# First head group's queries and keys as two interleaved sets of seven products, in a fused decoder layer on one core

## The chip, the cores and the metric

The kernel runs on one core of a Trainium2 chip. Its time is the device time of one execution in microseconds; the figure compared is the median over several runs. A profiled execution gives the trace from which all single durations come.

## The reference

One layer (batch 1, 512 positions, model width 1024, float32) with three branches that mix positions, gates, and a convolutional feed-forward network:

```python
u = rmsnorm(x, ln1_g)
proj = u @ w_in
q, k, v, pool_in, z, xbc, dt_raw, gate_pre = jnp.split(proj, split_idx, axis=-1)
y_a = dilated_attention_mixer(q, k, v, rel_bias) @ w_a        # 3 groups of 6 heads of 64
y_b = pool_mixer(pool_in, pool_w, pool_scale) @ w_b           # causal means over 2, 4, 8, 16
y_c = ssd_mixer(z, xbc, dt_raw, ...) @ w_c
gates = jax.nn.sigmoid(gate_pre + b_gate)
x = x + (gates[0] * y_a + gates[1] * y_b + gates[2] * y_c) @ w_o
x = x + conv_ffn(rmsnorm(x, ln2_g), ...)
return rmsnorm(x, final_g)
```

The change touches how the columns of `proj` for the first head group's queries and keys are computed: q and k of group 0 are each a product of u (512 x 1024) with 384 columns of `w_in`. Everything else is computed as before.

## The kernel before

**Products.** Every float32 operand is split into a high part (a cast to the format fp32r) and a low part (the operand less its high part). A product is three passes of TensorE: high weights by high x, high weights by low x, low weights by high x (`mm3`, L234). The normed x lies turned, with the model width on the partitions, as `uh` and `ul` in eight blocks of 128 rows by 512 positions. Most projections go by `chunk_a`: a tile of 128 columns of the weights is one accumulation of 3 x 8 matmuls of 128 x 512.

**Jobs and what runs ahead.** The work is a list of jobs, each a block of weights of up to 1 MB and a body with the matmuls. At the start of job n, VectorE makes the low part of the block of job n+1 (`wl`, L215), ScalarE is set to cast block n+2 (`wh`, L195), and SyncE's queue fetches block n+3 (`raw`, two buffers). TensorE, ScalarE, VectorE and GpSimd execute in the order in which the program is written; the DMA issues on SyncE's queue are ordered by the framework. Small pieces of other work (items) run between the products: `step()` advances each item in `running` to its next `yield`, and `after(n, item)` lets n steps pass first.

**The start.** x is loaded, its rows are normed and turned by TensorE, 256 positions at a time; `begin` (L1817) multiplies the first two weight blocks with each half as it comes. These two blocks and the two that follow, `weights[2]` and `weights[3]`, are the projections of the pool branch: eight chunks of 128 columns, two in a block. Each chunk is drained by `pool_evac`: ScalarE copies it out (`pu`, L926), GpSimd adds shifted copies (`psw`, L930 to L933: one addition for chunks 0 and 1, two for 2 and 3, three for 4 and 5, four for 6 and 7, with small copies beside them), and some steps later the item `later` makes the difference `pd` on VectorE (L939), its high part `pdh` on ScalarE (L941) and its low part `pdl` on VectorE (L942). Behind the pool projections come the values of group 0 (two jobs, matmuls of 128 x 400, tile `pb`), the queries and keys of group 0 (`qk_jobs(0)`, three jobs with a `q` and a `k` tile each, tile `pqk`), the pool's own products (`ppw`), the attention of group 0, and the output of the pool branch.

**Sevens.** The queries and keys of group 1 and some gates go by a scheme of Strassen's kind (`set_of_sevens`): the model width is cut into two halves of 4 blocks, the positions into two halves (`LO`, `HI`) and the columns into two sides, lefts (queries) and rights (keys). Seven products, named one to seven, of half the width, half the positions and one side's columns each take the place of eight. Each is, for each 128 columns of the side, 3 x 4 matmuls of 128 x 256. They need sums and differences of the quarters of x (`sums_of_u`: two `uf` that rebuild a block from its parts, four sums `sa` and `sb`, their high parts on ScalarE and low parts `sal`, `sbl` on VectorE; kept in `US`) and of the weights (`w`, L349, held in a pool `ypool` of two buffers). The sums of x are made once, during the output of the pool branch. The results are put together as they are drained: ScalarE copies `one`, `five`, `six` and `seven` out (L742), VectorE makes queries from `two` and keys from `six` and `seven` (the sinks, `q_sink` and `k_sink`, L694).

Of the kernel before, what the change touches and what calls it, by code (L numbers as in the profile page):

```python
# [13 lines left out]
OP = mybir.AluOpType  # L14
AX = mybir.AxisListType

P = 128
# [66 lines left out]
def trunk(ctx: ExitStack, tc, out, x, rel_bias, ln1_g, w_in, b_gate, w_a, pool_w, pool_scale, w_b,  # L84
# [469 lines left out]
    def grouped(ap, g):  # L554

        return ap.rearrange("p (r j) -> p r j", r=4)[:, :, ::-1]
# [4 lines left out]
    def plain(ap, g):  # L561
        return ap if g == 0 else ap.rearrange("p (r j) -> p r j", r=4)
# [114 lines left out]

    def q_sink(g, c):
        t = QK["q", g, c] = T(f"q{g}")
        half = lambda hi: grouped(t, g)[:, :, 64 * hi:64 * hi + 64]  # L680

        def two(ps, r):
            dve.scalar_tensor_tensor(half(0), turned_(ps), 0.125, turned_(r), OP.mult, OP.add)

        def four(ps):
            act.mul(half(1), turned_(ps), 0.125)

        return two, four

    def k_sink(g, c):  # L690
        t = QK["k", g, c] = T(f"k{g}")

        def put(hi, a, b):
            dve.tensor_tensor(plain(t, g)[:, :, 64 * hi:64 * hi + 64], turned_(a), turned_(b),  # L694
                              OP.subtract)

        return put

    def turned_(ap):
        return ap.rearrange("p (j r) -> p r j", r=4)  # L700

    ROLE, turn_of, due = {}, [0], []
# [7 lines left out]
    def set_of_sevens(lefts, rights, x, scales=(1.0, 1.0)):  # L710

        q = lambda two, c0: w_in[:, c0:c0 + P].rearrange("(k two p) c -> two p k c", two=2, p=P)[two]
        cols = [[c for c, _ in side] for side in (lefts, rights)]
        W, r, sinks = [], {}, {}
        role = {"two": "y", "five": "b", "three": "b"}

        def load():
            w = ypool.tile([P, 4, S], F32, name="w3", tag="xs")
            for h in range(2):
                W.append(w[:, :, 256 * h:256 * h + 256])  # L720
                for j, src in enumerate(quarter(0, h)):
                    sp.dma_start(W[h][:, :, src[0]:src[1]], src[2])

        def quarter(two, h):
            if cols[h][1] == cols[h][0] + P:
                c = cols[h][0]
                return [(0, 256, w_in[:, c:c + 256].rearrange("(k two p) c -> two p k c", two=2, p=P)[two])]
            return [(j * P, j * P + P, q(two, cols[h][j])) for j in range(2)]

        def bank(which):  # L730
            if not ROLE:
                for n in ("c", "y", "a", "b"):
                    ROLE[n] = MM("p")
            return ROLE[which]

        def cut(t, j):
            return t[:, 256 * j:256 * j + 256]

        def copy(ps, name, scales=(1.0, 1.0)):
            t = r[name] = T(name)  # L740
            if scales[0] == scales[1]:
                act.mul(t, ps, scales[0])  # L742
            else:
                for j in range(2):
                    act.mul(cut(t, j), cut(ps, j), scales[j])
            return t

        def use(name, ps):
            if name in ("two", "six"):
                for j, (_, make) in enumerate(lefts if name == "two" else rights):  # L750
                    sinks[name == "six", j] = make()
            if name == "one":
                copy(ps, "one", scales)
            elif name == "five":
                copy(ps, "five")
            elif name == "two":
                for j in range(2):
                    sinks[0, j][0](cut(ps, j), cut(r["one"], j))
            elif name == "six":
                t = copy(ps, "r2")  # L760
                for j in range(2):
                    sinks[1, j](0, cut(bank("b"), j), cut(t, j))
            elif name == "seven":
                t = copy(ps, "r7")
                for j in range(2):
                    sinks[1, j](1, cut(r["five"], j), cut(t, j))
            elif name == "four":
                for j in range(2):
# [19 lines left out]
        return load, sevens(lambda two, h: [src for _, _, src in quarter(two, h)], 256, W, body)  # L788

    def attend(g):  # L790
        nm, ls = both[:, :, :HEADS], both[:, :, 32:]
# [130 lines left out]
    def pool_evac(m, ps):  # L922
        g = m // 2
        w = 2 << g
        u = T("pu")
        act.copy(u, ps)  # L926
        cur, sh = u, 1
        while sh < w:
            nxt = T("psw")
            pool.tensor_tensor(nxt[:, sh:], cur[:, sh:], cur[:, :S - sh], OP.add)  # L930
            pool.tensor_copy(nxt[:, :sh], cur[:, :sh])
            cur, sh = nxt, sh * 2
        pool.tensor_tensor(cur[:, :w], cur[:, :w], ramp[:, g, :w], OP.mult)  # L933

        def later():
            yield
            yield
            d = T("pd")
            dve.scalar_tensor_tensor(d, cur, 1.0 / w, u, OP.mult, OP.subtract)  # L939
            dh, dl = T("pdh", F32R), T("pdl", F32R)  # L940
            act.copy(dh, d)  # L941
            dve.tensor_sub(dl, d, dh.bitcast(F32))  # L942
            DP[m] = (dh, dl)

        running.append(later())
# [1023 lines left out]
```

## Time and profile before

| | |
|---|---|
| median of 3 runs | 1025.87 us (1025.46 to 1026.5) |
| the profiled execution | 1026.25 us, its span 1024.5 us |
| mean granted TensorE clock | 0.998 |
| TensorE busy | 1014.8 us, 5396 matmuls |
| VectorE busy | 706.2 us, 967 instructions |
| ScalarE busy | 489.8 us, 821 instructions |
| GpSimd busy | 175.5 us, 143 instructions |

The span runs from the first to the last instruction of the profiled execution; its own time is 1.75 us longer. PE is TensorE's matrix engine, PEld its loading of weights (beside the matmuls), DVE is VectorE, ACT ScalarE, POOL GpSimd, SP SyncE. A timeline row gives start and busy time in us, engine, line, operation, output and inputs by their names in the program, shape, type, the count of instructions in the row, and in brackets the idle time ahead of it with what ended it.

### The profile page before, as it was taken

The numbers are of one execution on the slowest core, as the hardware profiler recorded it, in microseconds if no ns is written. First come the engines' busy times: TensorE is split into PE (matmuls) and PEld (weight loads), VectorE is DVE, ScalarE is ACT, GpSimd is POOL, SyncE is SP. The second block draws the span as 40 slices with busy tenths as digits, with TensorE's granted clock in tenths as the row PEclk, the third lists the DMA queues.
The fourth block names the chain that finished last, engine by engine and source line by source line (L and its number), as shares of the span: only waits on it lengthen the run. The fifth ranks groups of instructions, "written<-read, shape, count | busy, mean of one in ns | idle before, by whom it ended". The sixth has DMA issues, their size and how long they took to land.

```text
span 1024.5 us, 13696 instructions
## 1 busy us (share of the span) xinstructions
PE 1014.8 (99%) x5396; PEld 862.2 (84%) x5396; DVE 706.2 (69%) x967; ACT 489.8 (48%) x821; POOL 175.5 (17%) x143
## 2 busy tenths in 40 slices
PE   9999999999999999999999999999999999999997
PEld 9988878899998888888888888898888888888885
DVE  5562566776857758766768769767768677666775
ACT  6432455355546564567455235554454443443342
POOL 2680000011100004210143611202111011111120
PEclk9999999999999999999999999999999999999999
DMA  8444222147454234552253879342233224323142
GB/s 271 136 120 149 89 76 76 31 99 190 104 134 124 83 110 117 144 133 59 78 156 129 279 140 277 123 139 88 83 124 122 85 82 164 123 84 122 63 144 82
DMA packets 123055, 126.30 MB, mean 123 GB/s; under 512 B 5715, under 2 KB 104342, under 8 KB 122991
## 3 DMA queue, kind: packets, MB, share of 16 engines
q1 hardware_dynamic: 118015, 118.02, 36.8%
q0 software_dynamic: 4384, 6.55, 4.1%
q8 instruction: 42, 0.69, 0.3%
q10 hardware_dynamic: 592, 0.86, 0.2%
q14 instruction: 22, 0.18, 0.0%
HBM read 119.53 MB, written 2.22 MB: 119 GB/s over the span
## 4 chain that ended last, share of the span: by engine, by line
PE 95%; DVE 2%; DMA 1%; ACT 1%; issue 0%; ACTq 0%; DVEq 0%
PE pa L234 32%; PE pu L234 22%; PE p L234 19%; PE pqk L234 6%; PE pb L234 4%; PE pa L1817 2%; PE ps L813 1%; PE pu L1601 1%; PE ppw L234 1%; PE pt L841 1%; PE po L854 1%; PE py L1139 1%; DMA vr<-v 1%; DMA xin<-in_x_dram 1%; DVE wl L215 1%; PE pyo L1146 1%
## 5 line engine op out<-in xcount | busy, mean ns | idle before, releaser
L215 DVE TENSOR_TENSOR wl<-raw,wh 128x2048 fp32r<-128x2048 f32 (+3 forms) x89 | 196.8, 2212 | 40.4 <-ACT wh L195 31.0
L195 ACT CAST wh<-raw 128x1024 fp32r<-128x1024 f32 (+3 forms) x176 | 170.8, 991 | 43.4 <-DVE raw L339 26.1
L1462 DVE SCALAR_TENSOR_TENSOR hc<-pu,fcol,hc 128x510 f32<-128x510 f32 x88 | 65.8, 748 | 61.5 <-ACT hc L1459 59.8
L234 PE MATMUL pa<-uh,wh 128*128 128x512 f32 x336 | 86.5, 399 | 0.0
L234 PE MATMUL pu<-uh,wl 128*128 128x512 f32 (+1 forms) x352 | 83.7, 380 | 0.0
L234 PE MATMUL pu<-uh,wh 128*128 128x512 f32 (+1 forms) x352 | 83.5, 379 | 0.0
L234 PE MATMUL pu<-ul,wh 128*128 128x512 f32 (+1 forms) x352 | 83.5, 379 | 0.0
L234 PE MATMUL pa<-ul,wh 128*128 128x512 f32 x336 | 83.0, 389 | 0.0
L234 PE MATMUL pa<-uh,wl 128*128 128x512 f32 x336 | 83.0, 389 | 0.0
L1467 POOL TENSOR_TENSOR hc<-hc 128x512 f32<-128x512 f32 x22 | 32.3, 1468 | 272.7 <-DVE hc L1462 237.9
L234 PEld LDWEIGHTS pu<-uh,wl 128*128 128x128 f32 x352 | 64.1, 188 | 12.8 <-DVE wl L215 0.3
L234 PEld LDWEIGHTS pu<-ul,wh 128*128 128x128 f32 x352 | 64.2, 188 | 12.5
L234 PEld LDWEIGHTS pu<-uh,wh 128*128 128x128 f32 x352 | 64.1, 188 | 12.4
L234 PEld LDWEIGHTS pa<-ul,wh 128*128 128x128 f32 x336 | 63.1, 188 | 13.3
L234 PEld LDWEIGHTS pa<-uh,wl 128*128 128x128 f32 x336 | 63.1, 188 | 13.1
L234 PEld LDWEIGHTS pa<-uh,wh 128*128 128x128 f32 x336 | 61.2, 188 | 12.7 <-issue 0.7
L1459 ACT ACTIVATE hc<-pu,fcol,fcol 128x512 f32<-128x512 f32 x40 | 31.2, 780 | 81.0 <-PE pu L234 80.7
L195 ACT CAST wh<-w 128x512 fp32r<-128x512 f32 (+2 forms) x54 | 39.4, 770 | 25.2 <-DVE w L349 10.6
L215 DVE TENSOR_TENSOR wl<-w,wh 128x1024 fp32r<-128x1024 f32 (+2 forms) x27 | 43.1, 1595 | 8.8 <-ACT wh L195 6.7
L370 POOL DMA_DIRECT2D w<-in_w_in_dram x10 | 12.4, 1237 | 200.7 <-DVE w L349 173.9
L834 ACT ACTIVATE sb<-sb,both 128x128 f32<-128x128 f32 (+1 forms) x72 | 30.1, 419 | 31.8 <-DVE both L831 21.7
L1464 ACT ACTIVATE hc<-hc 128x512 f32<-128x512 f32 x22 | 13.9, 632 | 42.6 <-DVE hc L1462 42.6
(398 smaller groups left out, 1975.9 us busy)
## 6 DMA issues: line engine op xcount, KB each, us to landing
raw<-in_ffn_w_up_dram SPq DMA_DIRECT2D x22, 1024.0 KB
raw<-in_w_in_dram SPq DMA_DIRECT2D x21, 1024.0 KB
raw<-in_ffn_w_down_dram SPq DMA_DIRECT2D x11, 1024.0 KB
raw<-in_w_in_dram SPq DMA_DIRECT2D x20, 512.0 KB
raw<-in_w_b_dram SPq DMA_DIRECT2D x4, 1024.0 KB
al<-ad SPq DMA_DIRECT2D x16, 256.0 KB
raw<-in_w_c_dram SPq DMA_DIRECT2D x4, 1024.0 KB
w<-in_ffn_w_down_dram SPq DMA_DIRECT2D x4, 1024.0 KB
```

The lines of the kernel that those rows point to most:

```text
L195: act.copy(job.high[:, :, o], job.raw[:, :, o])
L215: (eng or dve).tensor_tensor(l[:, :, o], job.raw[:, :, o], h[:, :, o].bitcast(F32), OP.subtract)
L234: pe.matmul(ps, l, r, start=first and n == 0, stop=last and n == total - 1, skip_group_check=again)
L370: pool.dma_start(W[1][:, k:k + 2, at:at + n], src[:, k:k + 2, :], accum_op=OP.add)
L813: pe.matmul(pss[i][:, o:o + w * P], q[r, n * P:(n + 1) * P], k[r, kb * P:(kb + w) * P], start=True, stop=True)
L834: act.activation(sb[:, off:off + w * P], sb[:, off:off + w * P], AF.Exp, bias=nm[:, n, h:h + 1], accum_out=ls[:, n, h:h + 1])
L841: pe.transpose(pt[:, o:o + P], sb[:, o:o + P], eye)
L1459: act.activation(t, ps, AF.Identity, bias=ff["c1"][:, ff["b"] + m:ff["b"] + m + 1], scale=fw(2, m))
L1462: dve.scalar_tensor_tensor(t[:, sh:], ps[:, :S - sh], fw(k, m), t[:, sh:], OP.mult, OP.add)
L1464: act.activation(t, t, AF.Silu)
L1467: pool.tensor_tensor(a, a, t, OP.mult)
L1817: pe.matmul(first[2 * n + j][:, lo:hi], a[:, k, j * P:(j + 1) * P], b[:, k, lo:hi], start=a is wh and b is uh and k == 0, stop=a is wl and ...
```

## The change

The three jobs of `qk_jobs(0)` are replaced by two sets of sevens. The full set has the blocks 0 and 1 of the queries and keys (products of 24 matmuls of 128 x 256), the half set block 2 (`many` = 1, products of 12). The fourteen products are interleaved. The half set keeps `three` and `five` in a PSUM bank of its own (`p5`). The sums of x are made twice: behind the turning of x, for these two sets, and, as before, during the output of the pool branch for the sets of group 1. The sums that the first making keeps in `US` are dropped when the two sets are done. `later` of `pool_evac` waits 2 to 5 steps instead of 2. The weights that the sets hold in `ypool` are loaded during the pool projections; two more blocks of the full set are fetched during the value jobs (`ahead`). The matmuls of 128 x 512 become fewer by 144, those of 128 x 256 more by 252.

```diff
+    def ahead(jobs):
+        for job in jobs:
+            fetch(job)
+            job.load = lambda: None
...
     def set_of_sevens(lefts, rights, x, scales=(1.0, 1.0)):
...
+        many = len(lefts)
+        W, r, sinks, own = [], {}, {}, {}
+        z = "b" if many > 1 else "own"
+        role = {"two": "y", "five": z, "three": z}

         def load():
             w = ypool.tile([P, 4, S], F32, name="w3", tag="xs")
+            if many == 1:
+                for i, (two, h) in enumerate(((0, 0), (0, 1), (1, 0), (1, 1))):
+                    W.append(w[:, :, i * P:(i + 1) * P])
+                    sp.dma_start(W[i], q(two, cols[h][0]))
+                return
...
         def body(name, ws, parts):
...
-            for c in range(2):
+            for c in range(many):
...
     def pool_evac(m, ps):
...
         def later():
-            yield
-            yield
+            for _ in range((2, 2, 2, 2, 3, 3, 4, 5)[m]):
+                yield
...
     def program():
-        yield from jobs_a(w_in, C_POOL, 8, uhk, ulk, KD, pool_evac)
+        sets0 = [set_of_sevens(tuple((C_Q + i * P, lambda i=i: q_sink(0, i)) for i in blocks),
+                               tuple((C_K + i * P, lambda i=i: k_sink(0, i)) for i in blocks), x, (0.125, 0.125))
+                 for blocks, x in (((0, 1), "c"), ((2,), "a"))]
+        for i, job in enumerate(jobs_a(w_in, C_POOL, 8, uhk, ulk, KD, pool_evac)):
+            if i == 3:
+                yield Call(lambda: [load() for load, _ in sets0])
+            yield job
         yield Call(lambda: waiting.append(rows_of_bias()))
-        yield from v_jobs(0)
-        yield from qk_jobs(0)
+        for i, job in enumerate(v_jobs(0)):
+            yield job
+            if i == 0:
+                yield Call(lambda: ahead(sets0[0][1][n] for n in ("two", "three")))
+        for i, name in ((0, "one"), (0, "five"), (1, "one"), (0, "two"), (1, "five"), (0, "three"),
+                        (1, "two"), (1, "three"), (0, "six"), (1, "six"), (0, "seven"), (1, "seven"),
+                        (0, "four"), (1, "four")):
+            yield sets0[i][1][name]
+        yield Call(ROLE.clear)
+        yield Call(US.clear)
         yield from pool_out_job()
...
     begin(1, 0, 256, turns)
+    running.extend(after(n, sums_of_u(p)) for p, n in enumerate((0, 0, 1, 2)))
     turn()
     fetch(weights[2])
     fetch(weights[3])
```

Three places show what stands where in the engines' queues (line, operation, output and inputs, shape). Lines behind L172 are shifted in the changed kernel: L195 is L200 there, L215 L220, L926 L956, L939 and L942 are L969 and L972.

ScalarE, from the copies of the first pool chunks to the cast of the fourth weight block (the second `wh`), before:

```order
L926 COPY pu<-pa 128x512 x2
L195 COPY wh<-raw 128x2048
L926 COPY pu<-pa 128x512
L941 COPY pdh<-pd 128x512
L926 COPY pu<-pa 128x512
L941 COPY pdh<-pd 128x512
L195 COPY wh<-raw 128x2048
```

The same piece in the changed kernel:

```order
L956 COPY pu<-pa 128x512
L335 COPY sah<-sa 128x512
L336 COPY sbh<-sb 128x512
L335 COPY sah<-sa 128x512
L336 COPY sbh<-sb 128x512
L971 COPY pdh<-pd 128x512
L956 COPY pu<-pa 128x512
L335 COPY sah<-sa 128x512
L336 COPY sbh<-sb 128x512
L971 COPY pdh<-pd 128x512
L200 COPY wh<-raw 128x2048
```

Six casts of sums have come ahead of the fourth block's `wh`; it stands behind the second `pdh` in both.

VectorE, from the low part of the third weight block to that of the fourth, before:

```order
L215 TENSOR_TENSOR wl<-raw,wh 128x2048
L939 TENSOR_SCALAR pd<-psw,pu 128x512
L942 TENSOR_TENSOR pdl<-pd,pdh 128x512
L939 TENSOR_SCALAR pd<-psw,pu 128x512
L942 TENSOR_TENSOR pdl<-pd,pdh 128x512
L215 TENSOR_TENSOR wl<-raw,wh 128x2048
```

In the changed kernel, the part of it from the rebuilding of x (`uf`) to the second `pd`:

```order
L390 TENSOR_TENSOR uf<-uh,ul 128x512 x2
L969 TENSOR_SCALAR pd<-psw,pu 128x512
L972 TENSOR_TENSOR pdl<-pd,pdh 128x512
L338 TENSOR_TENSOR sal<-sa,sah 128x512
L339 TENSOR_TENSOR sbl<-sb,sbh 128x512
L338 TENSOR_TENSOR sal<-sa,sah 128x512
L339 TENSOR_TENSOR sbl<-sb,sbh 128x512
L329 TENSOR_TENSOR sa<-uf 128x256
L330 TENSOR_TENSOR sa<-sa,uf 128x256
L331 TENSOR_TENSOR sb<-uf 128x256
L332 TENSOR_TENSOR sb<-uf,sa 128x256
L969 TENSOR_SCALAR pd<-psw,pu 128x512
```

Four low parts and four sums stand between the first `pdl` and the second `pd`, and four more sums and two `uf` ahead of the first `pd`.

VectorE at the end of the sets, from the keys that come of `six` of the full set, through the low parts of the weights for `seven` and `four` (`wl` of 128 x 1024 for the full set, of 128 x 512 for the half set), in the changed kernel:

```order
L704 TENSOR_TENSOR k_1242<-p,r_1244 128x256
L704 TENSOR_TENSOR k_1243<-p,r_1244 128x256
L220 TENSOR_TENSOR wl<-w_729,wh 128x1024
L704 TENSOR_TENSOR k_1264<-p_1128,r_1265 128x256
L220 TENSOR_TENSOR wl<-w_732,wh 128x512
L704 TENSOR_TENSOR k_1242<-five,r_1298 128x256
L704 TENSOR_TENSOR k_1243<-five,r_1298 128x256
L220 TENSOR_TENSOR wl<-w_729,wh 128x1024
L704 TENSOR_TENSOR k_1264<-five,r_1320 128x256
L220 TENSOR_TENSOR wl<-w_732,wh 128x512
```

Before, the last jobs of the queries and keys had this in the same place of the queue:

```order
L672 COPY k_983<-pqk 128x512
L215 TENSOR_TENSOR wl<-raw,wh 128x2048
L672 COPY k_1044<-pqk 128x512
L215 TENSOR_TENSOR wl<-raw,wh 128x2048
L672 COPY k_1105<-pqk 128x512
L215 TENSOR_TENSOR wl<-raw,wh 128x2048
```

A `wl` still stands behind each drained `k`, but the tiles that it stands behind are halves, and three such pairs have become five.

More of the change, by code (lines that the diff above doesn't have):

```diff
@@ L679, in q_sink, with half @@
         t = QK["q", g, c] = T(f"q{g}")
[L680 removed]
+        def half(hi):
+            if g == 0:
+                return grouped(t, g)[:, 2 * hi:2 * hi + 2, :]
+            return grouped(t, g)[:, :, 64 * hi:64 * hi + 64]
         def two(ps, r):
[L683 removed]
+            dve.scalar_tensor_tensor(half(0), turned_(ps, g), 0.125, turned_(r, g), OP.mult, OP.add)
         def four(ps):
[L686 removed]
+            act.mul(half(1), turned_(ps, g), 0.125)
         return two, four
@@ L724, in quarter @@
         def quarter(two, h):
-            if cols[h][1] == cols[h][0] + P:
+            if many > 1 and cols[h][1] == cols[h][0] + P:
                 c = cols[h][0]
                 return [(0, 256, w_in[:, c:c + 256].rearrange("(k two p) c -> two p k c", two=2, p=P)[two])]
-            return [(j * P, j * P + P, q(two, cols[h][j])) for j in range(2)]
+            return [(j * P, j * P + P, q(two, cols[h][j])) for j in range(many)]
         def bank(which):
+            if which == "own":
+                if which not in own:
+                    own[which] = SM("p5")
+                return own[which]
             if not ROLE:
@@ L756, in use @@
             elif name == "two":
-                for j in range(2):
+                for j in range(many):
                     sinks[0, j][0](cut(ps, j), cut(r["one"], j))
@@ L760, in use @@
                 t = copy(ps, "r2")
-                for j in range(2):
-                    sinks[1, j](0, cut(bank("b"), j), cut(t, j))
+                for j in range(many):
+                    sinks[1, j](0, cut(bank(z), j), cut(t, j))
             elif name == "seven":
                 t = copy(ps, "r7")
-                for j in range(2):
+                for j in range(many):
                     sinks[1, j](1, cut(r["five"], j), cut(t, j))
             elif name == "four":
-                for j in range(2):
+                for j in range(many):
                     sinks[0, j][1](cut(ps, j))
@@ L786, in body @@
                 step()
-        return load, sevens(lambda two, h: [src for _, _, src in quarter(two, h)], 256, W, body)
+        jobs = sevens(lambda two, h: [src for _, _, src in quarter(two, h)], P * many, W, body)
+        if many == 1:
+            for i, name in ((2, "two"), (3, "three")):
+                jobs[name].load = lambda: None
+                jobs[name].form = lambda i=i: W[i]
+        return load, jobs
     def attend(g):
```

15 lines of the change are left out of this document (9 added, 6 removed).

## The prediction

> **What bounds the kernel now.** I read the page first, for the shares of the engines and the chain that ended last.
>
> ```profile
> span 1024.5 us, 13696 instructions
> PE 1014.8 (99%) x5396; PEld 862.2 (84%) x5396; DVE 706.2 (69%) x967; ACT 489.8 (48%) x821; POOL 175.5 (17%) x143
> PE 95%; DVE 2%; DMA 1%; ACT 1%; issue 0%; ACTq 0%; DVEq 0%
> ```
>
> TensorE is busy for 99% of the span and holds 95% of the chain. Next, what TensorE waits for (engine, line, releaser: microseconds, times, longest):
>
> ```profile
> PE pa L1774 <- DVE relb L507: 1.1, 1, 1.1
> PE p L234 <- DVE wl L215: 0.7, 2, 0.6
> ```
>
> These are its two largest waits, and neither lies at a place that the change touches. So at the start of the kernel, where the edit is, the product stream has no stall to lose: matmul time that goes is gained in full, and any operand that comes late is paid in full. Three questions follow: how much matmul time goes, which operands come late, what a stall costs beside itself.
>
> **Matmul time.** The timeline of TensorE (start, busy time, line, tiles, shape, count of a run of matmuls):
>
> ```profile
> 78.33 1.98 PE L234 MATMUL pqk<-uh,wh 128*128 128x512 f32 x8
> 110.97 0.62 PE L234 MATMUL ppw<-pdh,wh 128*128 128x512 f32 x2
> 241.20 0.64 PE L234 MATMUL p<-sah,wh 128*128 128x256 f32 x4
> 241.68 0.64 PE L234 MATMUL p<-sal,wh 128*128 128x256 f32 x4
> ```
>
> The first two rows enclose the queries and keys of the first group: 3 jobs x 2 tiles x 3 passes x 8 = 144 matmuls in 110.97 - 78.33 = 32.64 us, 226.7 ns each. The last two are from the existing sets of sevens: 4 matmuls of half width in 0.48 us, 120 ns each. The change puts 7 x 24 + 7 x 12 = 252 of these in their place: 252 x 0.120 = 30.24 us. That is **-2.40 us**: an eighth of the multiplications goes, but a half-width matmul takes 53% of a full one, not 50%.
> The Trainium skill ("TensorE: Matmul & The Clock Gate", Back-to-back issue gap) gives the gap of a single matmul as N/2.4 + 2.5 ns; by that the two would be 215.8 and 109.2 ns, and the term an estimated 31.08 - 27.51 = -3.6 us. The rows differ from it by 11 ns in both shapes, and the rows decide.
>
> **The second half of the pool projections.** VectorE and ScalarE run in program order. The sums of x, made a second time, put 32 instructions on VectorE (8 `uf`, which rebuild a block of x from its parts, 16 sums, 8 low parts) and 8 on ScalarE (their high parts) among the pool branch's evacuations, and ScalarE's cast of the fourth weight block now stands behind `pdh` of chunk 1, which waits for VectorE's `pd`. Before:
>
> ```profile
> 48.06 1.98 PE L234 MATMUL pa<-uh,wh 128*128 128x512 f32 x8
> 34.44 2.29 DVE L215 TENSOR_TENSOR wl<-raw,wh 128x2048 fp32r<-128x2048 f32 x1 [7.70 <-ACT wh L195]
> 39.41 0.68 DVE L939 SCALAR_TENSOR_TENSOR pd<-psw,pu 128x512 f32<-128x512 f32 x1
> 40.78 0.76 DVE L942 TENSOR_TENSOR pdl<-pd,pdh 128x512 fp32r<-128x512 f32 x1 [0.69 <-ACT pdh L941]
> 37.72 0.62 ACT L941 CAST pdh<-pd 128x512 fp32r<-128x512 f32 x1
> 40.65 1.91 ACT L195 CAST wh<-raw 128x2048 fp32r<-128x2048 f32 x1
> ```
>
> That cast ended at 42.56, and TensorE began with the block at 48.06: 5.5 us of slack. The first six `uf` and eight sums fall into VectorE's idle 7.70 us ahead of 34.44 and cost nothing. Behind the `wl` that ends at 36.73 there now stand four sums, two `uf`, `pd` and `pdl` of chunk 0, four low parts, four sums, and only then `pd` of chunk 1. Their durations, from where the same code runs later:
>
> ```profile
> 192.31 0.42 DVE L324 TENSOR_TENSOR sa<-uf 128x256 f32<-128x256 f32 x1
> 193.78 1.28 DVE L385 TENSOR_TENSOR uf<-uh,ul 128x512 f32<-128x512 f32 x2
> 715.03 0.68 DVE L333 TENSOR_TENSOR sal<-sa,sah 128x512 fp32r<-128x512 f32 x1
> 715.63 1.78 DVE L334 TENSOR_TENSOR sbl<-sb,sbh 128x512 fp32r<-128x512 f32 x1
> 715.28 1.58 POOL L1467 TENSOR_TENSOR hc<-hc 128x512 f32<-128x512 f32 x1 [4.13 <-DVE hc L1462]
> ```
>
> Four sums are 193.78 - 192.31 = 1.47 us; two `uf` 1.2 (1.28 less the overlap); `pd` to the end of `pdl` 41.54 - 39.41 = 2.1; a low part 0.60 from start to start. In all 1.47 + 1.2 + 2.1 + 2.4 + 1.47 + 0.68 = 9.3, so `pd` of chunk 1 ends at 46.0, against 40.09 before. Then 0.62 for `pdh` and 1.91 for the cast: 48.5, a wait of about 0.4 us. This is the lower bound, for VectorE alone.
> The last three rows show why it is more. GpSimd's operation, issued at 715.28 during `sal`, ends at 716.86, and `sbl`, issued behind `sal` at 715.63, takes 1.78 us where `sal` took 0.68: the two engines took turns, and VectorE lost 1.1. The same holds in the stretch at issue:
>
> ```profile
> 50.77 2.66 DVE L215 TENSOR_TENSOR wl<-raw,wh 128x1600 fp32r<-128x1600 f32 x1
> 61.78 1.81 DVE L215 TENSOR_TENSOR wl<-raw,wh 128x1600 fp32r<-128x1600 f32 x1
> 32.14 1.04 POOL L930 TENSOR_TENSOR psw<-pu 128x511 f32<-128x511 f32 x1 [17.38 <-ACT pu L926]
> ```
>
> The same `wl` takes 0.85 us more beside GpSimd, which there makes shifted sums of 1.04 us. Up to `pd` of chunk 1 GpSimd has one such sum of chunk 1, two each of chunks 2 and 3 to make: 5 x 1.04 = 5.2 us, and in a dense VectorE queue each costs a turn. Upper bound: 0.4 + 5.2 = 5.6; with its small copies too, some 7.4 by an estimate of 0.3 for each of six. I take **+5.5**, because both places nearest in kind, 50.77 and 715.63, show turns.
>
> **The first value job.** TensorE wanted its low part here:
>
> ```profile
> 60.41 0.90 PE L234 MATMUL pb<-wl,uh 128*128 128x400 f32 x4
> ```
>
> With the wait that is 65.9. VectorE has the cast of the fourth block at about 53.6; behind it stand `wl` (2.2), two low parts (1.2), `pd` to `pdl` (2.1), two low parts, `pd` to `pdl`, and the value job's `wl` (1.81): 64.1 in all, and with three or four more turns of GpSimd (chunks 4 and 5 have three sums each) 67 to 68. That is 0 to 2.1; I take **+1.5**.
>
> **The clock.** A stall this long may cost beside itself. At the start, and after the last matmul (window, busy times, granted clock, DMA share, GB/s):
>
> ```profile
> 1.06 6.74 PE L1774 MATMUL pa<-ones 128*128 128x128 f32 x38 [1.06 <-DVE relb L507]
> 7.64 1.95 PE L1834 MATMUL uT<-diag,xin 128*128 128x128 f32 x16
> 1019.50:1024.50 5.00, 0.00 (x0) 0.00 (x0) 1.18 (x5) 0.76 (x2) 0.00 (x0) 0.50 0.27 105
> ```
>
> The 16 take 122 ns each, the first 38 take 177: 2.1 us lost by a start from rest. In the last 5 us, without matmuls, the granted clock is 0.50. After 5.5 us of rest I therefore expect up to 2.1 us lost; since TensorE then arrives later at the value job's low part, 1.5 of it is the wait just counted. Net **+0.6** (0 if the stall is short).
> The Trainium skill (same page, Part 1, The HAM clock gate) has the clock halved after an idle window of some 3.4 us and restored after a busy one; by its window half of 3.4, an estimated 1.7 us, would be lost, and the net term 0.2. The start's 2.1 us bears it out in kind.
>
> **Waits inside the two sets.** The products of the half set last 12 x 0.12 = 1.44 us, shorter than what the full set's next product waits for. How a `six` or `seven` was drained before:
>
> ```profile
> 270.96 0.64 PE L234 MATMUL p<-sah,wl 128*128 128x256 f32 x4
> 271.64 0.60 ACT L742 ACTIVATE r<-p 128x512 f32<-128x512 f32 x1 [2.22 <-PE p L234]
> 272.27 1.17 DVE L694 TENSOR_TENSOR k<-p,r 128x256 f32<-128x256 f32 x2
> 273.36 2.44 DVE L215 TENSOR_TENSOR wl<-w,wh 128x1024 fp32r<-128x1024 f32 x2
> ```
>
> The product ends at 271.60, then the copy, two `k` results, and only behind them the next `wl`, 1.22 us long, ready at 273.36 + 1.22 = 274.58: 3.0 us after the product's end. In the change one half-set product and two passes lie between: 1.44 + 8 x 0.12 = 2.4. So 0.6, with the semaphores 0.7, at `seven` and again at `four` of the full set. `two` of the full set stands behind `pd` and `pdl` of the last pool chunk, and these behind ScalarE's copy of `five`: 0.60 + 0.62 + 0.69 + 1.22 = 3.2 for 2.4, so 0.8. `three` behind the `q` results and the pool output's `wl` behind `four` come within a few tenths; 0.3 for both by estimate. Sum **+2.5**; bounds 0 (GpSimd and VectorE both early) and 4 (each place a whole product late).
>
> **At nothing.** Two loads of weights now stand ahead of the pool's third and fourth block on SyncE's queue, 2 MB where 1.5 MB stood.
>
> ```profile
> 27.50:30.00 2.50, 2.50 (x23) 2.50 (x23) 0.00 (x0) 0.00 (x0) 0.00 (x0) 1.00 1.07 381
> 30.00:32.50 2.50, 2.50 (x23) 2.50 (x23) 0.00 (x0) 1.02 (x3) 0.36 (x1) 1.00 0.12 40
> ```
>
> The stream runs at 381 GB/s and is done just behind 30; 0.5 MB more is 1.3 us, before the cast of the third block at about 32.4. If it is not covered, it costs the difference, under 1 us. The value pair's loads move behind the pool output; they come 90 us ahead of use, so nothing waits. The extra evacuations in the sets (some 15 us on VectorE and ScalarE together) fit into idle time outside the places counted; the second making of the sums in the output branch is unchanged.
>
> **Sum.** -2.4 + 5.5 + 1.5 + 0.6 + 2.5 = +7.7 us. The profiled execution of before took 1026.25 us (span 1024.5 and 1.75 around it), the median of its runs is 1025.87; so 1033.95 for a profiled one and **1033.6 us** for the median.
>
> **Rivals.** *VectorE keeps the way.* Evidence for it:
>
> ```profile
> 390.14 2.28 DVE L215 TENSOR_TENSOR wl<-raw,wh 128x2048 fp32r<-128x2048 f32 x1
> 392.34 1.28 DVE L1115 TENSOR_TENSOR al<-al,cbt 128x512 f32<-128x512 f32 x2
> 391.47 3.32 POOL L1111 TENSOR_TENSOR xdl<-xd,xdh 128x512 fp32r<-128x512 f32 x1 [2.71 <-ACT xdh L1110]
> ```
>
> Here GpSimd stood still through `wl` and two `al`, and VectorE lost nothing (2.28 against 2.29). If it goes so, the wait for the fourth block is 0.4, no clock is lost, and the first value job is in time: -2.4 + 0.4 + 2.5 = +0.5, 1026.4 us, no measurable change. Against it stand the longer `wl` at 50.77 and `sbl` at 715.63. Chance 0.15.
> *Faster.* In addition the sets' waits vanish, which takes `wl` of `seven` and `four` ready 2.4 us after the product ahead and `pd` of chunk 1 ended by 45.6: -2.4 + 0 to 0.3, about 1023.6 us. The order of VectorE's queue speaks against it. Chance 0.10.
> *GpSimd blocks more than its turns.* Copies hold VectorE as well: 7.4 + 2.1 + 0.6 + 2.5 to 4 - 2.4 = +10.2 to +11.7: 1036.1 to 1037.6. Chance 0.15.
> The forecast case has 0.60; its own range, turns for three to six of the sums and 1.5 to 3.5 us in the sets, is 1030 to 1036. The range that leaves out the faster case and the last of the slow one is 1026.2 to 1037.5. A median of this kernel can tell about 0.2%, 2.05 us, from no change: below 1023.8 is faster, above 1027.9 slower. Faster 0.10, same 0.15, slower 0.75.
>
> **What would show it.** In the profile of after TensorE should wait at about 48 us for ScalarE's `wh` for 4 to 7 us, with a granted clock under 1 behind it; for `wl` of the first value job around 66 for 1 to 2 us; and three times 0.6 to 0.9 for `wl` between 85 and 120. The first `ppw` should start 7 to 9 us later than 110.97. I am wrong if TensorE does not wait near 48 us, if the stretch of the sets with its waits is shorter than 32.64 us by 2 us or more, or if a load is what it waits for.

## The result and the profile after

The changed kernel takes 1033.04 us (median of 6 runs, 1031.14 to 1033.93), the kernel before 1026.18 us beside it (6 runs): 6.86 us or 0.7% slower, ratio 1.0066 with a 95% interval of 1.0053 to 1.0079. The forecast was 1033.6.

The page of the changed kernel: span, busy time, chain. TensorE's busy time grew by 1.4 us, although 2.4 us of matmuls went (a matmul at a lowered clock counts as busy for longer), and 3% of the chain more lies outside it.

```profile
span 1031.1 us, 14049 instructions
PE 1016.2 (99%) x5504; PEld 867.4 (84%) x5504; DVE 739.9 (72%) x1022; ACT 502.9 (49%) x859; POOL 183.8 (18%) x147
PE 92%; DVE 3%; issue 2%; ACT 1%; POOL 1%; DMA 1%; SPq 0%; DVEq 0%; ACTq 0%; POOLq 0%
```

What TensorE waits for now: the wait for ScalarE's cast is new, that for the weights' low parts has grown from 0.7.

```profile
PE pa L239 <- ACT wh L200: 4.4, 1, 4.4
PE p L239 <- DVE wl L220: 1.4, 4, 0.7
```

Where it stands: TensorE's timeline, first two marks of before (start of the third weight block, of the values), then the same marks and the waits of after.

```profile
37.16 2.00 PE L234 MATMUL pa<-uh,wh 128*128 128x512 f32 x8
58.95 0.89 PE L234 MATMUL pb<-wh,uh 128*128 128x400 f32 x4
```

```profile
37.08 2.00 PE L239 MATMUL pa<-uh,wh 128*128 128x512 f32 x8
52.53 3.78 PE L239 MATMUL pa<-uh,wh 128*128 128x512 f32 x8 [4.38 <-ACT wh L200]
56.11 2.73 PE L239 MATMUL pa<-ul,wh 128*128 128x512 f32 x8
65.95 0.89 PE L239 MATMUL pb<-wh,uh 128*128 128x400 f32 x4
85.33 0.63 PE L239 MATMUL p<-uh,wh 128*128 128x256 f32 x4
94.30 0.74 PE L239 MATMUL p<-uh,wl 128*128 128x256 f32 x4 [0.66 <-DVE wl L220]
109.17 0.74 PE L239 MATMUL p<-sbh,wl 128*128 128x256 f32 x4 [0.21 <-DVE wl L220]
113.97 0.74 PE L239 MATMUL p<-uh,wl 128*128 128x256 f32 x4 [0.22 <-DVE wl L220]
117.42 0.63 PE L239 MATMUL ppw<-pdh,wh 128*128 128x512 f32 x2
```

With the marks 48.06, 78.33 and 110.97 of before, the time of each stretch comes out:

| stretch | before | after | difference |
|---|---|---|---|
| third weight block to fourth | 10.90 | 15.45 | +4.55 |
| fourth block to the values | 10.89 | 13.42 | +2.53 |
| values to queries and keys | 19.38 | 19.38 | 0.00 |
| queries and keys to the pool's products | 32.64 | 32.09 | -0.55 |
| all of it | 73.81 | 80.34 | +6.53 |

Behind that the two kernels run alike: the spans differ by 6.6. "All of it", from the third weight block to the first `ppw`, is the measure for the experiments too; it leaves out the start, which moved by up to 1.1 us between profiled executions (the third block began between 36.6 and 37.8).

The granted clock in the wait and behind it (window, busy times, clock):

```profile
48.00:52.50 4.50, 0.14 (x1) 0.00 (x0) 2.68 (x6) 2.44 (x3) 0.02 (x1) 0.81 0.01 2
52.50:58.70 6.20, 6.17 (x17) 4.88 (x18) 5.78 (x4) 2.64 (x5) 5.50 (x5) 0.59 0.45 134
```

The figures 0.81 and 0.59 are means. In windows of 0.1 us the clock is 1.00 or 0.50, and it is 0.50 from 50.82 to 57.64 us: it fell 2.7 us into the wait and came back 5.1 us behind it. The first 8 matmuls behind the wait stand 447 ns apart (52.53 to 56.11). Half of 5.1 us of work is lost, and that is the second stretch's +2.53.

What held the cast: VectorE's timeline of after, from the third block's `wl` to the `pd` of chunk 1, and ScalarE's cast.

```profile
34.36 3.15 DVE L220 TENSOR_TENSOR wl<-raw,wh 128x2048 fp32r<-128x2048 f32 x1 [0.32 <-POOL psw L963]
37.43 0.41 DVE L329 TENSOR_TENSOR sa<-uf 128x256 f32<-128x256 f32 x1
37.88 1.29 DVE L330 TENSOR_TENSOR sa<-sa,uf 128x256 f32<-128x256 f32 x1
39.43 1.25 DVE L332 TENSOR_TENSOR sb<-uf,sa 128x256 f32<-128x256 f32 x1
43.78 1.53 DVE L338 TENSOR_TENSOR sal<-sa,sah 128x512 fp32r<-128x512 f32 x1
45.84 1.52 DVE L338 TENSOR_TENSOR sal<-sa,sah 128x512 fp32r<-128x512 f32 x1
49.34 0.68 DVE L969 SCALAR_TENSOR_TENSOR pd<-psw,pu 128x512 f32<-128x512 f32 x1
50.58 1.89 ACT L200 CAST wh<-raw 128x2048 fp32r<-128x2048 f32 x1
```

`pd` of chunk 1 ends at 50.02, the cast at 52.47, TensorE begins at 52.53. Five operations take about 0.85 us longer than their like: `wl` 3.15 for 2.29, the two sums 1.29 and 1.25 for 0.41, the two `sal` 1.5 for 0.68. Each of them lies beside one of the five additions that GpSimd makes up to there (one of chunk 1, two each of chunks 2 and 3, from 34.33 to 46.81); beside GpSimd's small copies VectorE's operations keep their usual durations. That is 4.3 us of turns.

### The profile page after: what moved, and what is told of

Read it like the earlier page. It is cut to its first block, busy times and chain, and to the rows that moved or that the text cites. A ratio compares the mean times of both kernels' runs of the same rounds, so it can differ in the third digit from the quotient of the medians.

```text
span 1031.1 us, 14049 instructions
## 1 busy us (share of the span) xinstructions
PE 1016.2 (99%) x5504; PEld 867.4 (84%) x5504; DVE 739.9 (72%) x1022; ACT 502.9 (49%) x859; POOL 183.8 (18%) x147
## 4 chain that ended last, share of the span: by engine, by line
PE 92%; DVE 3%; issue 2%; ACT 1%; POOL 1%; DMA 1%; SPq 0%; DVEq 0%; ACTq 0%; POOLq 0%
PE pa L239 31%; PE p L239 23%; PE pu L239 22%; PE pb L239 4%; PE pqk L239 3%; PE ps L843 1%; PE pu L1631 1%; PE pt L871 1%; PE ppw L239 1%; PE po L884 1%; DVE wl L220 1%; PE py L1169 1%; DMA raw<-in_w_in_dram 1%; ACT wh L200 1%; PE pyo L1176 1%
## 5 line engine op out<-in xcount | busy, mean ns | idle before, releaser
L220 DVE TENSOR_TENSOR wl<-raw,wh 128x2048 fp32r<-128x2048 f32 (+3 forms) x88 | 192.9, 2193 | 32.4 <-ACT wh L200 22.7
L200 ACT CAST wh<-raw 128x1024 fp32r<-128x1024 f32 (+3 forms) x174 | 167.1, 980 | 46.7 <-DVE raw L344 26.0
L200 ACT CAST wh<-w 128x512 fp32r<-128x512 f32 (+3 forms) x78 | 50.3, 685 | 27.1 <-DVE w L354 10.0
L220 DVE TENSOR_TENSOR wl<-w,wh 128x1024 fp32r<-128x1024 f32 (+3 forms) x39 | 54.2, 1389 | 13.1 <-ACT wh L200 6.9
L375 POOL DMA_DIRECT2D w<-in_w_in_dram x14 | 17.2, 1230 | 190.1 <-DVE w L354 161.1
```

Of the source, the lines that this page charges most:

```text
L200: act.copy(job.high[:, :, o], job.raw[:, :, o])
L220: (eng or dve).tensor_tensor(l[:, :, o], job.raw[:, :, o], h[:, :, o].bitcast(F32), OP.subtract)
L375: pool.dma_start(W[1][:, k:k + 2, at:at + n], src[:, k:k + 2, :], accum_op=OP.add)
```

## Experiments

### The sums alone

```diff
 # the kernel before, with only:
     begin(1, 0, 256, turns)
+    running.extend(after(n, sums_of_u(p)) for p, n in enumerate((0, 0, 1, 2)))
```

> The kernel before with the early making of the sums of x alone added (nothing reads them; queries and keys as before). Theory: the sums alone put ScalarE's cast of the fourth weight block behind a late pd, so TensorE waits about 4.4 us at 48 us and then runs about 2.5 us slower under a lowered clock; nothing is gained later, so about 1033 us. Rival (the sets of sevens and their loads make the loss): no wait at 48 us, about 1026 us.

Measured 1033.11 us, ratio 1.0069 (1.0054 to 1.0084); the whole stretch took 118.05 - 37.46 = 80.59 us, as in the changed kernel. TensorE's timeline of this kernel:

```profile
37.46 2.00 PE L234 MATMUL pa<-uh,wh 128*128 128x512 f32 x8
52.92 3.78 PE L234 MATMUL pa<-uh,wh 128*128 128x512 f32 x8 [4.38 <-ACT wh L195]
118.05 0.62 PE L234 MATMUL ppw<-pdh,wh 128*128 128x512 f32 x2
```

The wait is the same 4.38 us. The early sums alone make the wait and the slow matmuls behind it; the sets of sevens, their loads and their evacuations have no part in those. In the changed kernel the sets gain 0.55 us against it, of the 2.40 that their matmuls save.

### Without GpSimd beside VectorE

```diff
     def pool_evac(m, ps):
...
         cur, sh = u, 1
-        while sh < w:
-            nxt = T("psw")
-            pool.tensor_tensor(nxt[:, sh:], cur[:, sh:], cur[:, :S - sh], OP.add)
-            pool.tensor_copy(nxt[:, :sh], cur[:, :sh])
-            cur, sh = nxt, sh * 2
-        pool.tensor_tensor(cur[:, :w], cur[:, :w], ramp[:, g, :w], OP.mult)
```

> The changed kernel without GpSimd's shifted sums and ramps in the pool branch (left out of the result; VectorE takes the plain copy instead). Theory (VectorE and GpSimd take turns, five of them of 0.85 us ahead of pd of chunk 1): the second pd ends near 45.8 us instead of 50.0, the cast near 48.2, the wait is 0.3 or less and no clock is lost: about 1026 us. Rival (VectorE's own queue is what is too long): pd of chunk 1 still ends after 49, wait over 3 us, about 1032 us.

This kernel leaves the causal means of the pool branch out. The stretch took 73.74 us, 6.6 less than in the changed kernel. The median was 1027.51 us, ratio 1.0012 (1.0003 to 1.0021), 1.5 us above what was expected, which the stretch doesn't account for (the profiled execution took 1026.54). VectorE's `pd` of chunk 1 and TensorE's fourth block:

```profile
45.59 0.69 DVE L963 SCALAR_TENSOR_TENSOR pd<-pu 128x512 f32<-128x512 f32 x1
48.80 2.14 PE L239 MATMUL pa<-uh,wh 128*128 128x512 f32 x8 [0.16 <-ACT wh L200]
```

`pd` ends at 46.28 instead of 50.02, and the wait shrinks from 4.38 to 0.16 us, though VectorE's own queue has every one of the sums. Counted from the start of the third weight block (37.57 here, 37.08 there) `pd` ends 4.23 us earlier, as much as the five turns add up to. So the queue by itself would just fit; the turns with GpSimd make the stall. The Trainium skill ("SBUF — State Buffer", Who interferes with whom) calls the port pair that the two engines share an exclusive lock; the trace agrees, with 0.85 us lost at a time.

### The cast moved ahead

```diff
     cast(weights[2])
+    cast(weights[3])
     low(weights[2])
     begin(1, 256, S)
-    cast(weights[3])
```

> The changed kernel with ScalarE's cast of the fourth weight block put directly behind that of the third, ahead of the pool's evacuations. Theory (ScalarE's order is the gate, VectorE's queue of sums and turns is the source): no wait at 48 us, but VectorE's low part of the block, still behind pd and pdl of chunk 1, ends near 53.7 where TensorE wants it at 51.8 (1.9 us), and the value job's low part is then some 2.6 us late; no lowered clock: about 1030.3 us. Rival (the cast's place alone makes the loss): no wait anywhere near, about 1026 us.

1029.47 us, ratio 1.0040 (1.0024 to 1.0055); stretch 77.92 in the profiled execution. There the sum was nearly met (+4.1 us in the stretch), its parts were not: TensorE's timeline and a window behind the wait.

```profile
50.42 1.97 PE L239 MATMUL pa<-ul,wh 128*128 128x512 f32 x8
55.16 3.32 PE L239 MATMUL pa<-uh,wl 128*128 128x512 f32 x8 [2.77 <-DVE wl L220]
58.27 2.42 PE L239 MATMUL pa<-uh,wh 128*128 128x512 f32 x8
```

```profile
55.00:58.50 3.50, 3.34 (x9) 2.66 (x10) 2.81 (x5) 0.72 (x2) 3.34 (x4) 0.61 0.59 191
```

The wait for the low part was 2.8 us, not 1.9 (GpSimd took a turn out of it too), and the clock fell all the same: 0.61 behind it, 16 matmuls in 60.53 - 55.16 = 5.37 us instead of 3.63. The value job, 2.6 us late by the expectation, was in time, because the slow matmuls covered it. This execution was the slowest of the four, 1031.68 us at a mean granted clock of 0.996; the other three took 1029.08 to 1029.77 us at 0.999, so the clock did not fall in each of them as it did here. ScalarE's order is thus the gate only; VectorE's queue is the source.

### Matmuls in the stall

```diff
                 prepare()
+            if n == 3:
+                busy = SM("busy")
+                for _ in range(18):
+                    pe.matmul(busy, weights[2].split[0][:, 0, :P], uh[:, 0, :], start=True, stop=True)
             job.body(job.split)
```

> The changed kernel with 18 idle matmuls of 128x512 (4.1 us, result not read) issued ahead of the fourth weight block, in the time in which TensorE waits. Theory (the clock falls in the stall): granted clock 1.00 behind the stall, the next 16 matmuls at 227 ns instead of 384, 2.5 us back, of which about 1.2 is lost again since the value job's low part is then late: about 1031.7 us. Rival (the slow matmuls come from something else, such as late weights): still slow, about 1033 us.

TensorE's timeline and the window behind the stall:

```profile
48.11 4.24 PE L1974 MATMUL busy<-uh,wh 128*128 128x512 f32 x18
52.68 2.11 PE L239 MATMUL pa<-uh,wh 128*128 128x512 f32 x8 [0.32 <-ACT wh L200]
66.31 1.00 PE L239 MATMUL pb<-wl,uh 128*128 128x400 f32 x4 [1.00 <-DVE wl L220]
```

```profile
52.60:58.20 5.60, 5.52 (x24) 4.60 (x25) 5.54 (x4) 2.30 (x5) 4.94 (x4) 1.00 0.36 109
```

The clock stays at 1.00, the fourth block runs at full speed, and the wait for the value job's low part, which nothing shows in the changed kernel, comes to light with 1.0 us. The stretch is 79.19 us, 1.15 shorter (1.3 was expected). The median, 1032.41 us, ratio 1.0061 (1.0046 to 1.0076), is 0.6 lower than the changed kernel's, within the scatter of both. So the 2.5 us are the clock's, and they hid a wait of 1.0, which costs 1.25 with the restart behind it (values to queries and keys 20.63 us instead of 19.38).

### The waits in the sets

keys_late puts the keys of `six` and `seven` behind the next low part, and the last `pd` behind `six` of the half set:

```diff
             elif name == "six":
                 t = copy(ps, "r2")
-                for j in range(many):
-                    sinks[1, j](0, cut(bank(z), j), cut(t, j))
+                def keys(b=bank(z), t=t):
+                    for j in range(many):
+                        sinks[1, j](0, cut(b, j), cut(t, j))
+                due.append(keys) if US_FIRST else keys()
... # the same for "seven"
-            for _ in range((2, 2, 2, 2, 3, 3, 4, 5)[m]):
+            for _ in range((2, 2, 2, 2, 3, 3, 4, 9)[m]):
```

(`US_FIRST` holds for the two sets of group 0 alone; lines that clear it behind them, and put what is still due, aren't shown.)

> The changed kernel with the sums where they are; in the two sets of group 0 the keys of six and seven are put behind the next low part, and pd of the last pool chunk four steps later, behind six of the half set. Theory: the waits of 0.66, 0.21 and 0.22 us in the sets go and no new ones come: the stretch of the sets takes 30.3 to 30.6 us instead of 32.1; the stall at 48 and the clock stay: about 1031.4 us. Rival (the waits are set by ScalarE or the banks): the stretch stays at 32.1, about 1033 us.

1030.11 us, ratio 1.0044 (1.0030 to 1.0057). TensorE's timeline, first product of the sets and first of the pool:

```profile
84.04 0.63 PE L239 MATMUL p<-uh,wh 128*128 128x256 f32 x4
114.27 0.63 PE L239 MATMUL ppw<-pdh,wh 128*128 128x512 f32 x2
```

The sets take 30.23 us: 252 matmuls at 120.0 ns and no wait. The order of VectorE's queue made all 1.86 us that the sets lost. Its stretch is 77.54 us, 2.80 under the changed kernel's. The other 0.9 of that is the clock, which cost 1.6 us in this profiled execution instead of 2.5 (the first 16 matmuls behind the stall in 57.41 - 52.19 = 5.22 us instead of 3.63); it lies ahead of all that the edit moves. How much of the median's fall is the clock's, one trace can't tell.

An earlier form, sets_free, had the last `pd` one step sooner (8 for 9), and the keys late in the sets of group 1 too; there it changes how the gates are put together, so that the gates of that group aren't the reference's.

> The changed kernel with the sums where they are, but in the sets the keys of six and seven are put behind the next low part (in the next product) and pd of the last pool chunk three steps later, behind three of the half set. Theory: the three waits in the sets (0.66, 0.21 and 0.22 us, and what their restart costs) go; the stall at 48 and the clock stay: the stretch of the sets takes 30.3 to 30.6 us instead of 32.1, about 1031.5 us. Rival (the waits are set by ScalarE or by the banks): the sets stay at 32.1, about 1033 us.

1030.73 us, ratio 1.0049 (1.0034 to 1.0063); the sets took 31.11 us (84.87 to 115.98), not 30.3 to 30.6, with two waits left:

```profile
106.34 0.74 PE L239 MATMUL p<-sah,wl 128*128 128x256 f32 x4 [0.21 <-DVE wl L220]
108.20 0.74 PE L239 MATMUL p<-sbh,wl 128*128 128x256 f32 x4 [0.16 <-DVE wl L220]
```

The last `pd` only met other low parts; one step later it met none.

### The sums spread out

`sums_early` does what `sums_of_u` does, with the step of each stage from a table: rebuilding, sums, high parts, low parts of the four pairs of blocks.

```diff
-    running.extend(after(n, sums_of_u(p)) for p, n in enumerate((0, 0, 1, 2)))
+    running.extend(sums_early(p) for p in range(4))
+SUMS_AT = ((1, 2, 7, 8), (1, 2, 8, 9), (2, 8, 9, 10), (9, 10, 11, 12))    # late_sums
+SUMS_AT = ((1, 2, 5, 6), (1, 2, 6, 7), (2, 5, 7, 8), (7, 8, 9, 10))       # late_sums_2
```

> The changed kernel with the sums' stages spread: rebuilding and sums in VectorE's idle time before 34 us as now, the rest behind the fourth weight block's low part, up to the end of the value jobs. Theory: no wait at 48 us, no lowered clock, the sets take 32.1 us as in the changed kernel: 1025.5 to 1026.3 us. Rival (the extra VectorE work must be paid somewhere in the dense stretch, as low parts of the value jobs or of the sets): waits of 2 us or more show up between 60 and 95 us, 1028 us or more.

1030.22 us, ratio 1.0042 (1.0025 to 1.0059), stretch 76.56: the theory's number was missed by 4 us. In the profiled execution there was no wait at 48 us and the clock stayed up, but the sums came too late for `five`, as the rival had it:

```profile
84.23 0.38 PE L239 MATMUL p<-sal,wh 128*128 128x256 f32 x1 [1.45 <-DVE sal L338]
85.97 0.74 PE L239 MATMUL p<-sah,wl 128*128 128x256 f32 x4 [1.35 <-DVE wl L220]
```

> As late_sums, but the high and low parts of the sums come 2 to 3 steps earlier, between the low part of the fourth weight block and that of the second value job. Theory: every low part is in time, only the waits inside the sets stay (1.4 us): no wait at 48, none at 84 to 86, about 1026 us. Rival (VectorE has no room for the sums at all before the sets): the wait turns up at the low parts of the value jobs, 2 us or more, about 1028 to 1030 us.

1026.97 us, ratio 1.0012 (1.0002 to 1.0022), stretch 74.89. One wait beside those that the sets had already was left, again 1.35 us for the low part of `five`. TensorE's row, and VectorE's timeline with what is ahead of it:

```profile
83.72 0.74 PE L239 MATMUL p<-sah,wl 128*128 128x256 f32 x4 [1.35 <-DVE wl L220]
76.01 0.69 DVE L338 TENSOR_TENSOR sal<-sa,sah 128x512 fp32r<-128x512 f32 x1 [2.99 <-POOL psw L982]
82.44 1.82 DVE L220 TENSOR_TENSOR wl<-w,wh 128x1024 fp32r<-128x1024 f32 x2 [0.73 <-ACT wh L200]
```

Ahead of `sal` VectorE stood idle for 2.99 us until a copy of GpSimd's shifted sums ended, whose data `sal` doesn't use.

### Both together

The run named both is late_sums_2 with sets_free's edit (the gates of group 1 as there).

> late_sums_2 and sets_free together. Theory: the two losses are independent, so the saving of 2.40 us of matmuls is all but gained: the sets in 30.3 to 30.6 us, no stall, 0.3 us at the pool's products: 1024 to 1024.5 us, faster than before. Rival (something else eats it): 1026 us or more.

1025.64 us, ratio 1.0001 (0.9992 to 1.0010), stretch 73.88: no stall, but late_sums_2's wait for `five` is still there, as are the two of sets_free. Level with before, not faster.

```profile
83.12 0.74 PE L239 MATMUL p<-sah,wl 128*128 128x256 f32 x4 [1.35 <-DVE wl L220]
```

combined has keys_late's edit and the last low parts at step 11.

> keys_late, and the sums' stages spread as in late_sums_2 but with the last low parts behind the first weights' low part of the sets. Theory: the low part for five is then in time too, so the sets take 30.3 to 30.6 us and the stretch from the third weight block to the pool's products 71.6 us (73.8 before): about 1024 us, 0.2% faster than before. Rival (VectorE and GpSimd have no room for the sums without a stall of 1 us or more): 1025.5 us or more.

1027.00 us, ratio 1.0015 (1.0006 to 1.0024), stretch 75.24. The low part for `five` was in time, and a new wait took its place, at the first product of the sets. Below it ScalarE's timeline and the window of the sets (busy times, clock):

```profile
80.31 0.74 PE L239 MATMUL p<-uh,wh 128*128 128x256 f32 x4 [2.09 <-ACT dtr L609]
79.70 0.48 ACT L607 COPY v<-pb 128x384 f32<-128x384 f32 x1 [8.35 <-POOL psw L987]
80.00:120.00 40.00, 39.62 (x285) 37.95 (x286) 28.49 (x36) 24.97 (x55) 5.06 (x4) 0.96 0.60 164
```

The wait of 2.09 us cost more than itself: the clock was 0.50 from 81.16 to 84.58 us, and the sets took 31.83 us (80.31 to 112.14) instead of 30.23 with no further wait in them. ScalarE's copy of the values waits 8.35 us for GpSimd, with which it shares no data; it shares the pool of 54 tiles. So I took six tiles out of that pool's traffic:

```diff
-        cur, sh = u, 1
+        cur, sh, two = u, 1, []
         while sh < w:
-            nxt = T("psw")
+            two.append(T("psw") if len(two) < 2 else two[-2])
+            nxt = two[-1]
```

> combined, and GpSimd's shifted sums of the later pool chunks go back and forth between two tiles instead of a new one for each addition, six fewer of the 54 shared tiles. Theory: in combined the value copy waited for a tile that GpSimd still held, not for VectorE's work; with the tile free no wait is left between 48 us and the pool's products, the sets take 30.2 us, and the stretch from the third weight block to the pool's products 71.4 to 72 us (73.8 before): about 1024 us, 0.2% under before. Rival (GpSimd itself ends too late, near 79 us, and something else waits for it): a wait of 1 us or more at the start of the sets again, 1025.5 us or more.

1026.76 us, ratio 1.0013 (1.0004 to 1.0022), stretch 75.07. The theory was missed again, by 2.8 us. The value copy no longer waits, but a `sal` does, and TensorE for `five` behind it:

```profile
78.92 0.69 DVE L338 TENSOR_TENSOR sal<-sa,sah 128x512 fp32r<-128x512 f32 x1 [2.80 <-POOL psw L988]
84.29 0.89 PE L239 MATMUL p<-sah,wl 128*128 128x256 f32 x4 [1.94 <-DVE wl L220]
```

Here too the clock fell behind the wait, to 0.50 from 84.72 to 88.13 us: the sets took 33.90 us, 1.94 of it the wait and some 1.7 the clock.

combined_3 moves the last low parts from step 11 to step 12.

> combined_2 with the low parts of the last sums three places further behind (behind pd and pdl of the pool's chunk 6 instead of ahead of them), where no shared tile that GpSimd's last chunk still holds is needed. Theory: with the wait for GpSimd's tile gone, VectorE has the low part for five some 1 to 2 us earlier, in time or 0.7 us late: the stretch from the third weight block to the pool's products 71.6 to 72.6 us (73.8 before), 1024 to 1024.8 us. Rival (VectorE beside GpSimd is simply full up to 80 us, so that each place of the sums makes something late): a wait of over 1 us between 59 and 86 us again, 1025.5 to 1027 us.

1025.01 us, ratio 0.9994 (0.9985 to 1.0003). TensorE's marks, and what VectorE waited for ahead of the wait that is left:

```profile
36.99 2.00 PE L239 MATMUL pa<-uh,wh 128*128 128x512 f32 x8
83.16 0.74 PE L239 MATMUL p<-sah,wl 128*128 128x256 f32 x4 [1.02 <-DVE wl L220]
109.66 0.63 PE L239 MATMUL ppw<-pdh,wh 128*128 128x512 f32 x2
78.70 0.69 DVE L996 SCALAR_TENSOR_TENSOR pd<-psw,pu 128x512 f32<-128x512 f32 x1 [2.81 <-POOL psw L988]
```

The stretch is 72.67 us, just outside the theory's 71.6 to 72.6, 1.14 under before and 7.7 under the changed kernel. That is the gain of 2.40 less 1.26, all of it the wait of 1.02 us for `five` and the restart behind it; the clock stayed at 1.00. Of the 2.40 us gained on combined_2, about 1.5 is thus the clock's. In the median it is 0.66 us, which this measurement can't tell from no change.

## Why the prediction was right, point by point

- **Matmuls, -2.40.** As forecast: 252 at 120.0 ns, seen bare in keys_late.
- **The fourth weight block, +5.5.** The place, the chain (`pd` of chunk 1, `pdh`, cast) and the mechanism (turns with GpSimd) were right; the wait was 4.4. I charged a turn with GpSimd's whole 1.04 us; VectorE lost 0.85 in each of five, 4.3 in all instead of 5.2. VectorE's own queue, put at 9.3 us, took 9.14 in no_shifts (37.14 to 46.28), and the lower bound of the wait, 0.4, measured 0.16. The five turns rule out the rival in which VectorE keeps the way, and that they account for the whole delay rules out the one in which GpSimd's copies block it too. One reading was off: the cast stood behind `pdh` of chunk 1 in the kernel before as well (40.12 and 40.65 us); new is only what stands ahead of `pd` in VectorE's queue.
- **The value job and the clock, +1.5 and +0.6.** Their sum of 2.1 was 2.53, but the split was the wrong way round: the whole of it showed as slow matmuls, and the value job's low part, 1.0 us late with the clock held up (fill), vanished behind them. The clock's loss was sized at 2.1 from the start of the kernel; behind the same wait it was 1.6 (keys_late) to 2.5 us.
- **The sets, +2.5.** 1.86 us, of which the waits are only 1.09. Their places were right, and `three` was in time; `two` waited 0.66, `seven` and `four` only 0.21 and 0.22 where I had 0.7 each: the two `k` results ran in 0.76 us, where the row that I took them from, which puts the positions in another order, showed 1.17:

```profile
107.23 0.76 DVE L704 TENSOR_TENSOR k<-p,r 128x256 f32<-128x256 f32 x2 [0.81 <-ACT r L767]
```

  The other 0.77 us I had not counted: about 0.25 lost at the restart behind each of three waits, as behind the waits of 1.0 us in fill and combined_3. That this term came out nearer to +2.5 than its waits is luck.

- **At nothing.** TensorE waits for no load in the stretch: right.
- **The sum.** +7.7 was +6.53 in the stretch: the wait with its restart 1.0 too high (4.55 for 5.5), the sets 0.6 too high, the value job and the clock 0.4 too low.
- **The signs.** The wait near 48 us and the lowered clock came as told. The wait at the first value job didn't, only one of the three waits in the sets was as long as told, and the first `ppw` came 6.45 us later than 110.97, not 7 to 9.
- **The rival "faster"** needed the sets without waits and `pd` of chunk 1 by 45.6. keys_late brought about the first, the runs that spread the sums the second (`pd` of chunk 1 ended at 40.45 us in late_sums_2; no_shifts, with 46.28, just missed it), and combined_3 both but for one wait of 1.02 us. Its stretch is shorter than that of before: the conditions were the right ones, and in the changed kernel the order of VectorE's queue beside GpSimd kept them from being met.

My first guess at a remedy fell: late_sums was to cost next to nothing and cost 2.75 us in the stretch. The time from 37 to 80 us, with VectorE and GpSimd both busy, has little room left for the sums, and the pool of tiles seems to tie further work to GpSimd's pace. That a shared tile is what `sal` and the value copy waited for is inferred: the wait moved when six tiles left the traffic, and the `pd` at 78.70 us in combined_3 waited for a copy of chunk 7 although the sums of chunk 6 that it reads were done at 69.72, which leaves its own new tile. It was not shown for each tile. Whether the last 1.0 us can be had too stays open.

## What to carry to other kernels

In a kernel whose matrix engine never waits, first look what a saving asks of the engines beside it, and where in the program: here 2.4 us of matmuls cost 32 small VectorE instructions, which would have fitted by their own durations, all but 0.16 us, but not beside GpSimd. Count a turn for each of GpSimd's large additions in a dense stretch of VectorE. Price a wait of TensorE above its length: here 0.25 us for the restart, and 1.6 to 2.5 where the clock fell. When the gate of a stall is moved and not its source (the cast, the sums), look for the next thing in the queue that is late, and for tiles that one engine gives back to another.

## What the runs showed that I had not expected

- The lowered clock has one length. In the profiled executions the granted clock was 0.50 for 3.41 us or for twice that, and the loss is half of the part of it in which TensorE works. The loss is measured as what the block or the set behind the wait took beyond its time at full clock, the wait left out:

| run | wait, its end (us) | clock 0.50 (us) | of it in work | measured loss |
|---|---|---|---|---|
| the changed kernel | 4.38, 52.53 | 50.82 to 57.64 | 5.1 | 2.5 |
| sets_free | 4.39, 52.24 | 50.20 to 57.03 | 4.8 | 2.4 |
| sums_only | 4.38, 52.92 | 50.54 to 57.36 | 4.4 | 2.2 |
| keys_late | 4.38, 52.19 | 51.93 to 55.34 | 3.2 | 1.6 |
| cast_first | 2.77, 55.16 | 55.75 to 59.16 | 3.4 | 1.7 |
| combined | 2.09, 80.31 | 81.16 to 84.58 | 3.4 | 1.6 |
| combined_2 | 1.94, 84.29 | 84.72 to 88.13 | 3.4 | 1.7 |

- The same wait of 4.38 us cost 1.6 to 2.5 us, by the moment at which the clock fell: 2.7 us into it in the changed kernel, 4.1 in keys_late. Behind the three shorter waits it fell only when TensorE worked again. The length of the wait alone doesn't decide: in late_sums TensorE was idle for 2.8 of 3.2 us (82.78 to 85.97) and the clock stayed at 1.00. What sets the moment no run here shows. The Trainium skill ("TensorE: Matmul & The Clock Gate", Part 1, The HAM clock gate) names an idle window of about 3.4 us; here waits of 1.94 to 2.77 us were enough in three traces.
- Filling the wait with matmuls whose result nobody reads kept the clock at 1.00 at no cost of its own.
